# Moving a head's attention scores beside the previous head's values in a decoder layer

## The chip, the cores and the metric

The kernel runs on one core of a Trainium2 chip. The metric is device microseconds of one execution, as the median of several. TensorE (PE) multiplies; ScalarE (ACT), VectorE (DVE) and GpSimd (POOL) do the rest, and SyncE (SP) and POOL issue most transfers.

## The reference

One decoder layer over 256 tokens of width 2048, in float32. The input is normalised and projected. One branch is multi-head latent attention with 16 heads (128 plain and 64 rotary dimensions for queries and keys, 128 for values); the other a gated convolution over three tokens. Both are projected, merged by sigmoid gates, projected once more, normalised and added to the input.

```python
h = _rmsnorm(x, pre_norm_g)
proj = jnp.einsum('bsd,de->bse', h, w_in)
(q_a, c_kv, k_rope, z_mla, c_in, b_gate, c_gate, z_conv, g_mla, g_conv) = jnp.split(proj, cuts, axis=-1)
q = jnp.einsum('bsr,re->bse', _rmsnorm(q_a, q_a_norm_g), w_q_b)
kv = jnp.einsum('bsr,re->bse', _rmsnorm(c_kv, kv_a_norm_g), w_kv_b)
# ... split into heads, rotary positions on q_rope and k_rope
attn = _causal_mla_attention(q_nope, q_rope, k_nope, k_rope, v)
attn = attn.reshape(b, s, MLA_WIDTH) * jax.nn.silu(z_mla)
y_mla = jnp.einsum('bse,ed->bsd', attn, w_o_mla)
u = c_gate * c_in
u_pad = jnp.pad(u, ((0, 0), (CONV_K - 1, 0), (0, 0)))
conv = sum(conv_w[k] * u_pad[:, k:k + s] for k in range(CONV_K))
y_conv = jnp.einsum('bse,ed->bsd', b_gate * conv * jax.nn.silu(z_conv), w_o_conv)
merged = jax.nn.sigmoid(g_mla) * y_mla + jax.nn.sigmoid(g_conv) * y_conv
x = x + _rmsnorm(jnp.einsum('bsd,de->bse', merged, w_out), post_norm_g)
```

## The kernel before

Every float32 product is made from two rounded parts, hi and lo: hi is a copy on ACT, lo the rest of a subtraction on DVE (`split_act`, L242 to L249; the lines L243 and L244 carry most of both engines' work). A product is then three matmuls.

Weights come as a fixed list of units, `plan`, of 1 MB each (2048 columns), numbered in the order of use. `take(i)` (L213) hands out unit i; before that, `ahead` loads units up to three further on and splits the next one. A unit is split in two halves of 1024 columns, into tiles `whi` and `wlo` with five buffers each. So a half can be split only once PE has finished the half five places before it. Loads go through SP's queue.

The middle of the kernel is a loop over the 16 heads (L779 to L855). A head's turn in the loop has four units of the convolution branch, `channels(h, 0)` to `channels(h, 3)`, of 24 matmuls each; they are filler for PE around the attention work and not tied to the head. Four heads make a group with its own four units of `gates` ahead of the first head of the group (`at == 0`). Heads come in pairs: in the first of a pair the rotary queries of the next pair are made (`group_r`), in the second its plain queries and keys (`group_a`).

A head's attention has four steps. `score(h)` (L775) calls `scores` (L599): eight matmuls into the one PSUM bank of tag `st`, then mask, maximum, exponential and sum on DVE and ACT, a transposition into `via` on DVE, and four transfers from POOL's queue into DRAM (`go`). `arrive()` (L772) issues, on POOL's queue, the transfer that brings the oldest waiting tile back (`come`), here the turned probabilities `p`. `turn` (L642) splits them into `pt`, hi on ACT and lo on DVE. `values(h, pt)` (L649) makes four matmuls into the one bank of tag `o`.

Before, `score(h)` stood at the head's start, in front of its first unit (for head 0 behind it; head 15's in head 14 behind the second unit). Its `turn` came in the next head behind the second unit, and `values` behind the third; in a group's first head the previous head's `turn` and `values` stand between the gate units instead.

The convolution's taps (`taps`, L734) shift tokens by transfers on POOL's queue, load three rows of tap weights (`cw`, two buffers) on the same queue, and multiply and add on DVE (L756); `next(tap)` runs the next step. `channels_done` (L709) scales what a head's four units made and so frees the two PSUM banks of tag `cv`.

The program is built with a scheduler that orders each engine's instructions by its own estimate of when they are ready. Matmuls and POOL's transfers keep the order in which they are written. `turn`'s two instructions are pinned behind what was written just before them on their engines (`keep_in_program_order`), but what is written later may still be put in front of them. On the chip each engine runs its queue in the order built.

Of the kernel before, what the change touches and what calls it, by code (L numbers as in the profile page):

```python
# [23 lines left out]
H = 16  # L24
# [58 lines left out]
def tile_layer(ctx: ExitStack, tc: tile.TileContext, xw, w0, xb, x, pos, pvec, post_g, wc, wz, wcv, wkr, wqk, wqr, wv, cwr, wsq, out):  # L83
# [129 lines left out]
    def take(i):  # L213
        ahead(i)
        parts = splits.pop(i)

        def piece(j, n):
            o = j * n
            h, o = o // HALF, o % HALF
            return parts[h][0][:, o : o + n], parts[h][1][:, o : o + n]  # L220

        return piece

    def bank(name, tag="mm", bufs=4):
        return psum.tile([P, 512], F32, name=name, tag=tag, bufs=bufs)
# [80 lines left out]
    def temp(name, shape=(P, S), dt=F32, bufs=2, tag=None):  # L306

        tag, n = tag or name.rstrip("0123456789_"), shape[-1]
        if n % LINE == 0:
            return bp.tile(list(shape), dt, name=name, tag=tag, bufs=bufs)  # L310
        return bp.tile([P, -(-n // LINE) * LINE], dt, name=name, tag=tag, bufs=bufs)[:, :n]
# [78 lines left out]
    def whole(dst, ps):  # L390

        t = temp("half")
        nc.scalar.activation(t[:, :], ps[:, S:], AF.Copy)
        nc.vector.tensor_tensor(dst, ps[:, :S], t[:, :], op=ALU.add)
# [98 lines left out]
    def latent_split(name, both, g):  # L493

        f = lat_f[name].rearrange("p t (i k x) -> p k t i x", i=4, k=KR)
        for k in range(KR):
            hi, lo = (both[:, k, o : o + S].rearrange("p (t i x) -> p t i x", t=NT, i=4) for o in (0, S))
            tc.keep_in_program_order(nc.scalar.activation(hi, f[:, k], AF.Copy, scale=col(g, k)))
            tc.keep_in_program_order(
                nc.vector.scalar_tensor_tensor(lo, f[:, k], col(g, k), hi.bitcast(F32), op0=ALU.mult, op1=ALU.subtract)  # L500
            )
# [33 lines left out]
    def key_rope():  # L535
        rows(kr_f)
        rope(kr_f, kr_f, True)
        split_act(kr[:, 0, :], kr[:, 1, :], kr_f)
# [57 lines left out]
    def make(i, j):  # L596
        {"a": group_a, "r": group_r, "v": group_v}[i](j)
# [44 lines left out]
    def turn(p):  # L642

        pt = temp("pt", (P, 2, 3 * P), F32R, 1)
        hi, lo = (pt[:, j : j + 1, :].rearrange("p o (k q) -> p (o k) q", k=3) for j in range(2))
        split_act(quarters(hi), quarters(lo), by_rows(p[:, :], 3), True)
        return pt

    def values(h, pt):  # L649
        vv = groups["v", h // HV]  # L650
        j = h % HV
        o = bank(f"o{h}", tag="o", bufs=1)
        vs = slice(j * DV, (j + 1) * DV)
        both = o[:, :].rearrange("p (i q) -> p i q", i=2)
        mm = matmul
        mm(both, vv[0][:, 0, vs], pt[:, :, :S], start=True, stop=False)
        mm(o[:, :S], vv[1][:, 0, vs], pt[:, 0, :S], start=False, stop=False)
        mm(o[:, P:S], vv[1][:, 1, vs], pt[:, 0, S:], start=False, stop=False)
        mm(both[:, :, P:], vv[0][:, 1, vs], pt[:, :, S:], start=False, stop=True)

        at = at_t[:, h // HV, :, :].rearrange("p t (i k x) -> p t i k x", i=4, k=HV)[:, :, :, j, :]
        f = temp("f")
        whole(f[:, :], o)
        nc.vector.tensor_tensor(at, f[:, :].rearrange("p (t i x) -> p t i x", t=NT, i=4), at, op=ALU.mult)
# [5 lines left out]
    def quarter(pss, w, i):  # L670

        for t in range(NT):
            for k4 in range(4):
                k = 4 * i + k4
                a = [x_both[:, k, o + t * P : o + (t + 1) * P] for o in (0, S)]
                product(pss[t][:, :], a, w(k4, 512), k == 0, k == KD - 1)

    def gates(v, i):
        if i == 0:
            z_ps["now"] = [bank(f"z{v}_{t}") for t in range(NT)]  # L680
        quarter(z_ps["now"], take(u_gate[v][i]), i)

    def gates_done(v):
        for t in range(NT):
            ps, g, r = z_ps["now"][t], at_t[:, v, t, :], r_col[:, t : t + 1]
            nc.scalar.activation(g, ps[:, :], AF.Sigmoid, scale=r)
            now = nc.vector.scalar_tensor_tensor(g, ps[:, :], r, g, op0=ALU.mult, op1=ALU.mult)
            if v == 0:
                tc.keep_in_program_order(now)

    def gates_turn(v, t):
        g = at_t[:, v, t, :]
        go, come = turned(g, temp("cw", (P, 512), bufs=2), 4)
        go()
        return lambda: come(g)
# [5 lines left out]
    def channels(h, i):  # L701

        if i == 0:
            cv_ps["now"] = [bank(f"cv{h}_{t}", tag="cv", bufs=2) for t in range(NT)]
        quarter(cv_ps["now"], take(u_head[h][i]), i)
        if i == 3:
            channels_done(*divmod(h, 4))

    def channels_done(j, n):  # L709
        for t in range(NT):  # L710
            ps, r = cv_ps["now"][t], r_col[:, t : t + 1]
            w, u = cv_w[:, t, :], cv_t[:, j, t, :]
            if n == 0:
                nc.scalar.activation(u, ps[:, :], AF.Copy, scale=r)
            elif n == 1:
                nc.vector.scalar_tensor_tensor(u, ps[:, :], r, u, op0=ALU.mult, op1=ALU.mult)
            elif n == 2:
                nc.scalar.activation(w, ps[:, :], AF.Copy, scale=r)
            else:
                g = temp("cg", (P, 512), bufs=1)  # L720
                nc.scalar.activation(g[:, :], ps[:, :], AF.Sigmoid, scale=r)
                nc.vector.scalar_tensor_tensor(g[:, :], ps[:, :], r, g[:, :], op0=ALU.mult, op1=ALU.mult)
                nc.vector.tensor_tensor(w, w, g[:, :], op=ALU.mult)
# [48 lines left out]
    def arrive():  # L772
        coming.pop(0)()

    def score(h):  # L775
        ps_by_head[h], come = scores(h)
        coming.append(come)

    for h in range(H):  # L779
        v, at = divmod(h, HV)  # L780

        if at == 0:
            for i in range(4):
                gates(v, i)
                if v == 0 and i == 0:
                    ckv_come()
                elif v == 0 and i == 1:
                    next(table_parts)
                    key_rope()
                elif v == 0 and i == 2:  # L790
                    latent_split("qa", qa, "q_g")
                elif v and i == 0:
                    arrive()
                elif v and i == 1:
                    pt = turn(ps_by_head.pop(h - 1))
                    next(tap)
                elif v and i == 2:
                    values(h - 1, pt)
                    make("v", v)
            if v:  # L800
                next(tap)
            else:
                latent_split("ckv", ckv, "kv_g")
            gates_done(v)
        if h == 0:

            ahead(u_grp["r", 0])
            for i in first:
                make(*i)
            channels(h, 0)  # L810
        if h < H - 1:
            score(h)
        if h:
            channels(h, 0)
        if at == 0:
            coming.append(gates_turn(v, 0))
        channels(h, 1)
        if at == 0:
            arrive()
            coming.append(gates_turn(v, 1))  # L820
        else:
            pt = turn(ps_by_head.pop(h - 1))
        if h == H - 2:
            score(h + 1)

        if at == 2 or h == H - 1:
            next(tap)
        if at and h < H - 1:
            arrive()
        channels(h, 2)  # L830
        if at:
            values(h - 1, pt)
        else:
            arrive()
            if v:
                coming.append(channels_join(v - 1, 0))
        for i in made[h]:
            make(*i)
        if h == H - 1:
            pt = turn(ps_by_head.pop(h))  # L840
        channels(h, 3)
        if at == 2 or h == H - 1:
            next(tap)
        while coming and h < H - 1:
            arrive()
        if h == H - 1:
            values(h, pt)
        if at == 3:
            coming.append(channels_join(v, 1))
        if at == 1:  # L850
            tap = taps(v, 1)
            next(tap)
        elif at == 3 and h + 1 < H or h == H - 2:
            tap = taps(v, 0)
            next(tap)  # L855
# [280 lines left out]
```

## Time and profile before

| | |
|---|---|
| Median of three runs | 1035.57 us (1035.38 to 1036.19) |
| The profiled execution, its time and its span | 1035.04 us and 1033.3 us |
| PE busy, matmuls | 1026.6 us (99%), 4680 |
| DVE, ACT, POOL busy | 682.0 us (66%), 526.5 us (51%), 180.5 us (17%) |
| Mean granted TensorE clock | 0.999 |

Shares are of the span. Times in the views are microseconds from the start of the span; a mean of one instruction is in nanoseconds. A line of a timeline gives start, length, engine, line of the kernel, operation, output and input, and in brackets how long the engine was idle before it and what released it. In a list of groups, the numbers behind the bar are busy time, mean, and idle time before.

### The profile page before, as it was taken

The numbers are of one execution on the slowest core, as the hardware profiler recorded it, in microseconds if no ns is written. First come the engines' busy times: TensorE is split into PE (matmuls) and PEld (weight loads), VectorE is DVE, ScalarE is ACT, GpSimd is POOL, SyncE is SP. The second block draws the span as 40 slices with busy tenths as digits, with TensorE's granted clock in tenths as the row PEclk, the third lists the DMA queues.
The fourth block names the chain that finished last, engine by engine and source line by source line (L and its number), as shares of the span: only waits on it lengthen the run. The fifth ranks groups of instructions, "written<-read, shape, count | busy, mean of one in ns | idle before, by whom it ended". The sixth has DMA issues, their size and how long they took to land.

```text
span 1033.3 us, 12729 instructions
## 1 busy us (share of the span) xinstructions
PE 1026.6 (99%) x4680; PEld 855.2 (83%) x4680; DVE 682.0 (66%) x957; ACT 526.5 (51%) x734; POOL 180.5 (17%) x345
## 2 busy tenths in 40 slices
PE   9999999999999999999999999999999999999997
PEld 7888888888888888888888888888888888888886
DVE  7588777777777677867867785564455455455562
ACT  7766545555455454564555565344434444443551
POOL 4640421104201142112313120020010001002000
PEclk9999999999999999999999999999999999999999
DMA  9775866558665685757776765565566557558642
GB/s 358 282 252 215 274 214 227 205 219 287 193 253 187 209 302 188 282 179 244 251 248 224 262 219 201 203 221 189 202 215 210 189 201 242 180 191 334 232 165 81
DMA packets 44670, 233.25 MB, mean 226 GB/s; under 512 B 7968, under 2 KB 10656, under 8 KB 21696
## 3 DMA queue, kind: packets, MB, share of 16 engines
q1 hardware_dynamic: 32544, 199.67, 54.6%
q0 software_dynamic: 11632, 29.48, 8.5%
q10 hardware_dynamic: 432, 3.29, 0.8%
q8 instruction: 36, 0.59, 0.2%
q14 instruction: 26, 0.21, 0.1%
HBM read 215.66 MB, written 12.58 MB: 221 GB/s over the span
## 4 chain that ended last, share of the span: by engine, by line
PE 99%; DVE 0%; ACT 0%; issue 0%; POOL 0%; POOLq 0%
PE cv L88 34%; PE sq L88 34%; PE out L88 8%; PE z L88 8%; PE qn L88 2%; PE kn L88 2%; PE qa L88 2%; PE vv L88 2%; PE ckv L88 2%; PE sc L88 1%; PE qr L88 1%; PE o L88 1%; PE idle L88 0%; PE kr L88 0%; DVE og L989 0%; ACT junk L970 0%
## 5 line engine op out<-in xcount | busy, mean ns | idle before, releaser
L244 DVE TENSOR_TENSOR wlo<-raw,whi 128x1024 fp32r<-128x1024 f32 (+1 forms) x370 | 440.2, 1196 | 282.4 <-ACT whi L243 271.8
L243 ACT ACTIVATE whi<-raw 128x1024 fp32r<-128x1024 f32 (+1 forms) x372 | 382.6, 1035 | 403.4 <-PE sq L88 180.4
L88 PE MATMUL cv<-whi,x_both 128*128 128x512 f32 x1024 | 321.1, 389 | 0.0
L88 PEld LDWEIGHTS cv<-whi,x_both 128*128 128x128 f32 x1024 | 192.3, 188 | 39.2
L88 PE MATMUL cv<-wlo,x_both 128*128 128x512 f32 x512 | 199.5, 390 | 0.0
L88 PE MATMUL sq<-whi,x_both 128*128 128x512 f32 x512 | 158.3, 389 | 0.0
L88 PEld LDWEIGHTS sq<-whi,x_both 128*128 128x128 f32 x512 | 96.1, 188 | 20.0
L88 PEld LDWEIGHTS cv<-wlo,x_both 128*128 128x128 f32 x512 | 96.2, 188 | 19.0
L88 PE MATMUL sq<-wlo,x_both 128*128 128x512 f32 x256 | 99.6, 389 | 0.0
L88 PE MATMUL z<-whi,x_both 128*128 128x512 f32 x256 | 79.9, 389 | 0.0
L88 PE MATMUL sq<-whi,at_both 128*128 128x512 f32 x256 | 79.5, 389 | 0.0
L88 PE MATMUL sq<-whi,cv_both 128*128 128x512 f32 x256 | 79.5, 389 | 0.0
L88 PE MATMUL out<-whi,m_both 128*128 128x512 f32 x256 | 79.0, 389 | 0.0
L326 POOL DMA_DIRECT2D far<-sg x32 | 17.6, 555 | 312.5 <-DVE sg L318 238.4
L326 POOL DMA_DIRECT2D far<-via x64 | 35.4, 559 | 182.2 <-DVE via L318 182.2
L88 PEld LDWEIGHTS sq<-whi,at_both 128*128 128x128 f32 x256 | 48.1, 188 | 10.0
L88 PEld LDWEIGHTS sq<-whi,cv_both 128*128 128x128 f32 x256 | 48.1, 188 | 10.0
L88 PEld LDWEIGHTS z<-whi,x_both 128*128 128x128 f32 x256 | 48.1, 188 | 10.0
L88 PEld LDWEIGHTS out<-whi,m_both 128*128 128x128 f32 x256 | 48.1, 188 | 9.9
L88 PEld LDWEIGHTS sq<-wlo,x_both 128*128 128x128 f32 x256 | 48.1, 188 | 9.9
L88 PE MATMUL z<-wlo,x_both 128*128 128x512 f32 x128 | 49.8, 389 | 0.0
L88 PE MATMUL sq<-wlo,at_both 128*128 128x512 f32 x128 | 49.8, 389 | 0.0
(217 smaller groups left out, 1126.5 us busy)
## 6 DMA issues: line engine op xcount, KB each, us to landing
raw<-wsq_dram SPq DMA_DIRECT2D x80, 1024.0 KB, 4.8
raw<-wcv_dram SPq DMA_DIRECT2D x64, 1024.0 KB, 5.7
raw<-wz_dram SPq DMA_DIRECT2D x16, 1024.0 KB, 4.8
raw<-wqk_dram SPq DMA_DIRECT2D x8, 1024.0 KB, 6.6
cw<-cwr_dram POOLq DMA_DIRECT2D x24, 256.0 KB, 6.0
raw<-wc_dram SPq DMA_DIRECT2D x4, 1024.0 KB, 10.0
raw<-wv_dram SPq DMA_DIRECT2D x4, 1024.0 KB, 5.1
far<-via POOLq DMA_DIRECT2D x64, 48.0 KB, 3.3
```

Of the source, the lines that this page charges most:

```text
L88: return tc.keep_in_program_order(nc.tensor.matmul(*a, **kw))
L243: a = nc.scalar.activation(hi, src, AF.Copy)
L244: b = nc.vector.tensor_tensor(lo, src, hi.bitcast(F32), op=ALU.subtract)
L326: tc.keep_in_program_order(queue.dma_start(out=f[i], in_=m))
```

## The change

The score of a head moves from its start to behind the third unit of the convolution, in front of the previous head's values. In the first head of a group it moves between the gate units, in front of the same values there, and its transfer back is issued at the end of the gates. Head 0's score moves behind its third unit, head 15's from behind the second unit of head 14 to the end of that head. The transfer back of the other scores, issued before behind the second unit, is now issued at the end of the head (L844's loop), head 15's behind the second unit of head 15.

```diff
@@ the gate units of a group's first head
                     next(tap)
                 elif v and i == 2:
+                    score(h)
                     values(h - 1, pt)
                     make("v", v)
...
             gates_done(v)
+            if v:
+                arrive()
         if h == 0:
...
             for i in first:
                 make(*i)
-            channels(h, 0)
-        if h < H - 1:
-            score(h)
-        if h:
-            channels(h, 0)
+        channels(h, 0)
         if at == 0:
             coming.append(gates_turn(v, 0))
         channels(h, 1)
...
         else:
             pt = turn(ps_by_head.pop(h - 1))
-        if h == H - 2:
-            score(h + 1)
 
         if at == 2 or h == H - 1:
             next(tap)
-        if at and h < H - 1:
+        if h == H - 1:
             arrive()
         channels(h, 2)
+
+        if h == 0 or at and h < H - 1:
+            score(h)
         if at:
             values(h - 1, pt)
...
         while coming and h < H - 1:
             arrive()
+        if h == H - 2:
+            score(h + 1)
         if h == H - 1:
             values(h, pt)
```

## The prediction

> **What bounds the kernel now.** I read the page first: its busy times and the chain that ended last.
>
> ```profile
> span 1033.3 us, 12729 instructions
> PE 1026.6 (99%) x4680; PEld 855.2 (83%) x4680; DVE 682.0 (66%) x957; ACT 526.5 (51%) x734; POOL 180.5 (17%) x345
> PE 99%; DVE 0%; ACT 0%; issue 0%; POOL 0%; POOLq 0%
> ```
>
> PE is busy for 1026.6 of 1033.3 us and carries the chain by itself. Next, the waits of PE alone (engine, line, releaser, total, times, longest):
>
> ```profile
> PE idle L88 <- POOL mhalf L264: 1.0, 1, 1.0
> PE fin L88 <- ACT dg L1011: 0.9, 1, 0.9
> ```
>
> Between the first microsecond and the last product PE waits for nothing. So the change can gain almost nothing: it neither removes nor shortens a matmul, and there is no wait to remove. It can lose wherever something PE needs comes late, and each such wait is paid in full. A microsecond or two (0.2%, 2.1 us) is about what a measurement of this kernel can tell from no change.
>
> The chain in order of time (start, length, what) gives the rhythm around the change:
>
> ```profile
> 245.20 0.94 PE sc L88 x8
> ...
> 291.98 1.40 PE qr L88 x8
> ...
> 316.13 0.57 PE o L88 x4
> ...
> 584.32 5.48 PE cv L88 x24
> 589.80 0.57 PE o L88 x4
> ```
>
> A score (sc) is 0.94 us of PE, a head's values (o) 0.57, a rotary query group (qr) 1.40, a unit of the convolution 5.48. Values need `pt`, the turned probabilities, split on ACT (hi) and then DVE (lo). The timelines of ACT and DVE show how early that is ready today, and the order in which the queues hold it:
>
> ```profile
> 280.24 0.51 ACT L243 ACTIVATE pt<-p 128x384 fp32r<-128x384 f32 x1
> ...
> 316.17 1.06 ACT L243 ACTIVATE whi<-raw 128x1024 fp32r<-128x1024 f32 x1 [0.24 <-PE cv L88]
> ...
> 571.60 1.06 ACT L243 ACTIVATE whi<-raw 128x1024 fp32r<-128x1024 f32 x1 [2.50 <-PE cv L88]
> 572.57 0.51 ACT L243 ACTIVATE pt<-p 128x384 fp32r<-128x384 f32 x1
> ```
>
> ```profile
> 572.69 1.23 DVE L244 TENSOR_TENSOR wlo<-raw,whi 128x1024 fp32r<-128x1024 f32 x1 [1.01 <-ACT whi L243]
> 573.83 0.55 DVE L244 TENSOR_TENSOR pt<-p,pt 128x384 fp32r<-128x384 f32 x1
> ```
>
> The `pt` of 280.24 serves a product some 10 us later. The row at 316.17 is a weight split whose buffer was freed by the unit that PE ended at 316.13: such splits stand in ACT's queue and run 0.04 us after PE lets go. The last two rows of ACT and the two of DVE are the pattern that I price below: a weight split in front of `pt` on both engines. From the start of the first (571.60) to the end of `pt`'s lo part (573.83+0.55 = 574.38) takes 2.78 us.
>
> **The change, part by part.** The PE work is the same to the instruction. In the changed program's built order the score of heads 1 to 14 (bar 4, 8, 12, which get it beside the values in the gate units) stands directly in front of the preceding head's values; head 0's stands behind its third unit, head 15's at the end of head 14. The matmuls' own cost: nothing.
>
> *The time the softmax has.* Before, a score stood at the head's start and its `pt` was turned six units later; now about three units and the group's products lie between. How long the path takes, for the score at 245.20 (DVE, then POOL; the last row is from the answer for tile p):
>
> ```profile
> 242.72 1.71 DVE L460 TENSOR_TENSOR rp_b<-f,sin_t 32x256 f32<-32x256 f32 x4
> ...
> 254.84 0.57 DVE L318 STREAM_TRANSPOSE via<-p 128x384 f32<-128x384 f32 x1
> ```
>
> ```profile
> 255.71 2.20 POOL L326 DMA_DIRECT2D far<-via  x4 [5.54 <-DVE via L318]
> 259.87 0.57 POOL L330 DMA_DIRECT2D p<-far  x1 [1.96 <-DMA far<-via]
> ...
> DMA to landing us min/median/max: 2.7/4.3/6.7
> ```
>
> PE ends that score at 246.14; `via` is done at 255.41 (9.3 us); `p` is sent for at 259.87 and lands 4.3 later (2.7 to 6.7): 18 us in all. (The row at 242.72 is the rotation of a query group, 1.71 us of DVE.) Most turns now have 18 us to the place where they stand and another unit before PE wants them. These are hidden by that unit, 5.48 us. Two places are not, because the queues are fixed when the program is built and the scheduler has put the turn late:
>
> ```
> ACT: ... whi65_0  pt(6)  sc_half(7)  half(o6) ...      DVE: ... wlo65_0  pt(6) ...
> DVE: ... cg(15,1)  wlo115_0  mv1+mv2  cv_w  cv_f*cw  pt(15) ...
> ```
>
> *Heads 2, 6 and 10.* Unit 65 is five half buffers behind head 7's third unit (62), so `whi65_0` can only start when PE ends that unit. PE goes on with sc7 (0.94 us) and then wants o6, which waits for `pt(6)` behind that split on both engines: 0.04 + 2.78 − 0.94 = 1.9 us of waiting. Head 2 (unit 40) and head 10 (unit 90) have the same order: 3 × 1.9 = 5.6 us. This is a lower end, for `p` itself is late here: the built order puts the rotation (1.7 and its two sums), two tap products and the values' sums among the softmax steps on the DVE, some 6 us together, so I count 15.6 us from the score's start to `via` (an estimate), then by the rows above 0.3 + 2.2 + 2.0 + 4.3 to the landing: 24.4. `pt`'s turn comes at 25.7 (0.94 + 0.57 + 1.40 + four units = 24.7, and 1.0 for `whi`). With the slowest landing (6.7) it is 1.1 us more each: 5.6 to 8.9. I take 5.6, the median landing.
>
> *The last values, o15.* PE ends the last convolution unit at 589.80 in both programs, but for the waits above (the same matmuls are before it). What stands in front of `pt(15)`, with its times before (ACT, DVE, POOL timelines, and the page's DMA issues: KB each, median us to landing):
>
> ```profile
> 589.83 0.69 ACT L721 ACTIVATE cg<-cv,r_both 128x512 f32<-128x512 f32 x1 [0.30 <-PE cv L88]
> 590.42 1.05 ACT L243 ACTIVATE whi<-raw 128x1024 fp32r<-128x1024 f32 x1
> ```
>
> ```profile
> 593.25 0.69 DVE L756 TENSOR_TENSOR cv_f<-cv_f,cw 128x512 f32<-128x512 f32 x1
> ```
>
> ```profile
> 571.74 0.52 POOL L747 MEMSET mv<- 1x512 f32 x1 [5.25 <-DVE cv_f L756]
> ...
> 573.77 1.11 POOL L740 DMA_DIRECT2D cw<-cwr_dram  x2
> ...
> cw<-cwr_dram POOLq DMA_DIRECT2D x24, 256.0 KB, 6.0
> ```
>
> Before, `pt(15)` ran in front of all this. Now `pt`'s lo part follows the tap's product with the third `cw` (593.25 before), with two more tap joins of about 0.6 inserted: 593.25 + 1.2 + 0.6 = 595.05, end 595.6. PE waits from 589.80: 5.8 us. On POOL the transfers of head 15's score now stand in front of that tap's transfers. Its score ends on PE at 567.4 (589.80 less four units and o14, 0.57); with 9.3 us to `via`, 0.3 + 2.2 for the four issues and 2.0 for the shift's two fills and copies (571.74 to 573.77), the first `cw` is sent for at 581.3 instead of 573.77 and lands 6.0 later, at 587.3. The third reuses its buffer and waits for the first product (587.9), is sent for at 588.2 to 588.9 and lands near 595: 0.6 us later than the DVE wants it. Sum 6.4, ends 5.8 (the DMA in time) and 8.5 (each landing a us slower).
>
> *The clock.* What a pause of that length does is seen only at the end (PE timeline; windows by columns PE, PEld, DVE, ACT, POOL, granted clock, DMA share, GB/s) and at the start (PE groups):
>
> ```profile
> 1027.35 1.13 PE L88 MATMUL fin<-og,dg 128*128 128x256 f32 x4 [0.87 <-ACT dg L1011]
> ...
> 1031.00:1032.00 1.00, 0.00 (x0) 0.00 (x0) 0.00 (x0) 0.00 (x0) 0.00 (x0) 1.00 0.42 156
> 1032.00:1033.30 1.30, 0.00 (x0) 0.00 (x0) 0.00 (x0) 0.00 (x0) 0.00 (x0) 0.51 0.00 0
> ...
> L88 PE MATMUL idle<-ones 128*128 128x128 f32 x16 | 3.8, 430 | 1.0 <-POOL mhalf L264 1.0
> ...
> L88 PE MATMUL fin<-xr,ident 128*128 128x256 f32 x4 | 1.0, 378 | 0.0
> ```
>
> The last matmul ends at 1028.5; the clock is whole until 1032 and half after it: 3.5 us of idling lose it. The first sixteen matmuls, of 128 columns, take 430 ns each, more than 378 for 256 columns late in the kernel: about 3.8 us at half clock at the start. A 6.4 us wait is longer than 3.5, so I expect half clock behind o15 for about as long as at the start: 3.8 us of work at half speed, 1.9 us lost (ends 0 and 3.8). The waits of 1.9 us lose none. [...] No row here shows a pause in mid-kernel.
>
> *Table loads.* Exponentials now fall between the gates' sigmoids and those of the next head: 18 loads in the built order instead of 12. One load, with the exponential behind it (ACT timeline):
>
> ```profile
> 228.16 1.28 ACT L630 ACT_TABLE_LOAD   x1
> 229.46 0.40 ACT L630 ACTIVATE p<-p,nb 128x128 f32<-128x128 f32 x1
> ```
>
> Six of 1.28 us on ACT, which idles for half of the span; the next instruction starts at once. I take nothing for PE. [...]
>
> *The DVE behind the third unit.* In odd heads the score's steps, 3 us of DVE, now stand in front of the product that frees the convolution's PSUM banks (L716), which the next head's first unit needs:
>
> ```profile
> 275.03 0.74 DVE L716 SCALAR_TENSOR_TENSOR cv_f<-cv,r_both,cv_f 128x512 f32<-128x512 f32 x1
> ```
>
> It ended at 275.77; the second bank is wanted half a unit (2.7) behind 275.05, at 277.8. Spare 2.0 us, and the DVE is idle a third of the span by the page (66% busy) to take up the 3: about 1 us stays, an estimate. Cost 0; 1 us for each of heads 1, 5, 9, 13 if the cover is gone.
>
> Sum: 5.6 + 6.4 + 1.9 = 13.9 us. The profiled execution took 1035.04 (span 1033.3), 0.5 under the median of 1035.57. Against the median: 1049.5 us.
>
> **The rivals.** (1) *The clock stays whole.* The trace shows one loss, at its end, with thin work ahead of it (0.87 us idle before 1027.35); between dense products a pause may have to be longer than 6.4, or mine is shorter than I count. Then 5.6 + 6.4: 1047.6. Against it: 6.4 is well over 3.5.
>
> (2) *More waits.* The crowded DVE also lets the banks (4 us for four heads) or `p` at heads 2, 6, 10 (3.3) come late. 1053 to 1057; with the first price 1053.5. For it: spares of about 1 us worked out by hand; against it: weights are split two units ahead.
>
> (3) *Not slower.* `pt` comes in time, as the row at 280.24 shows for today, and PE never waits. It would need DVE and ACT to do `pt` before the splits that stand in front of it, that is, those splits freed at least 1.9 us earlier and o15's chain 5.8 us earlier. The time is then that of before, less what a change of shape between products might cost: a score's 1920 columns at the convolution's pace (5.48 us for 24 x 512) are 0.86 us, 0.08 under its 0.94, 1.3 for sixteen: 1034.3. The built order speaks against it; nothing but an error in my reading of it speaks for it.
>
> (4) *The turns alone*, with o15's chain in time: 1041.2. Against it: `pt(15)` is behind a split that PE itself frees at 589.80.
>
> **How the numbers follow.** Forecast 0.48; rival 1 0.22; rival 2 0.18; rival 4 0.06; rival 3 0.06. The range reaches from rival 1 with one turn in time and the short o15 wait (3.7 + 5.8: 1045.0) to rival 2 with half of each price (1049.5 + 2 + 1.6) and the slow end of o15 (2.1), 1055.5; outside lie rivals 3, 4 and the tail of 2. Slower by over 0.2%: 0.93; rival 3 is mostly within 0.2% (0.05); faster by more (0.02) has no wait to come from.
>
> **What would show it.** The waits of PE, empty today, should name DVE's L244 for o: three of about 1.9 us near 182, 318 and 454 (right behind the scores of heads 3, 7 and 11) and one of about 6 us from about 595 on. The granted clock should be below 1 for a few us behind the last. PE's busy time should grow by no more than the half-clock stretch; table loads by six. I am wrong if PE's waits stay empty, if they sit at weight splits (whi, wlo) or at cv's first matmul instead of o, or if the long one is under 3 us.

## The result

| | before | after |
|---|---|---|
| Median of six executions each | 1035.70 us (1035.38 to 1036.78) | 1051.72 us (1051.24 to 1053.91) |
| The profiled execution and its span | 1035.04 us, 1033.3 us | 1051.91 us, 1050.1 us |

The ratio after to before is 1.0159 (95% interval 1.0148 to 1.0170): slower by 16.0 us. The forecast was 1049.5 with a range from 1045.0 to 1055.5.

The page of the changed kernel, its busy times and the chain that ended last:

```profile
PE 1030.9 (98%) x4680; PEld 857.6 (82%) x4680; DVE 680.7 (65%) x957; ACT 535.4 (51%) x740; POOL 179.6 (17%) x345
PE 89%; POOL 3%; DVE 3%; issue 3%; ACT 1%; DVEq 0%; POOLq 0%; ACTq 0%
```

The same 4680 matmuls, six more instructions on ACT (the table loads), and PE no longer carries the chain alone. Its waits (engine, line, releaser, total, times, longest):

```profile
PE o L88 <- DVE pt L244: 11.9, 4, 5.8
PE idle L88 <- POOL mhalf L264: 1.0, 1, 1.0
PE fin L88 <- ACT dg L1013: 0.9, 1, 0.9
PE cv L88 <- DVE wlo L244: 0.4, 1, 0.4
```

The second and third were there before. New are the last, 0.4 us of which more below, and the first; PE's timeline gives its four places: the values of heads 2, 6, 10 and 15 wait for `pt`.

```profile
184.85 0.54 PE L88 MATMUL o<-pt,vv_hi 128*128 128x512 f32 x1 [2.04 <-DVE pt L244]
...
323.03 0.47 PE L88 MATMUL o<-pt,vv_hi 128*128 128x512 f32 x1 [2.04 <-DVE pt L244]
...
459.63 0.47 PE L88 MATMUL o<-pt,vv_hi 128*128 128x512 f32 x1 [2.04 <-DVE pt L244]
...
604.69 0.76 PE L88 MATMUL o<-pt,vv_hi 128*128 128x512 f32 x1 [5.81 <-DVE pt L244]
```

The queues of ACT and DVE in front of o6 (323.03) show why:

```profile
320.10 1.06 ACT L243 ACTIVATE whi<-raw 128x1024 fp32r<-128x1024 f32 x1 [0.24 <-PE cv L88]
321.07 0.51 ACT L243 ACTIVATE pt<-p 128x384 fp32r<-128x384 f32 x1
```

```profile
319.89 2.53 DVE L244 TENSOR_TENSOR wlo<-raw,whi 128x1024 fp32r<-128x1024 f32 x2 [2.86 <-ACT whi L243]
322.34 0.55 DVE L244 TENSOR_TENSOR pt<-p,pt 128x384 fp32r<-128x384 f32 x1
```

ACT idles 0.24 us until PE gives up a buffer, splits the weights, and only then `pt`; on DVE `pt` stands behind the halves of `wlo`, and PE starts 0.14 us after `pt`'s lo part ends (322.89). In front of o15 on ACT and DVE:

```profile
601.47 0.52 ACT L243 ACTIVATE pt<-p 128x384 fp32r<-128x384 f32 x1 [0.92 <-DMA p<-far]
```

```profile
601.05 1.21 DVE L244 TENSOR_TENSOR wlo<-raw,whi 128x1024 fp32r<-128x1024 f32 x1
602.19 0.68 DVE L756 TENSOR_TENSOR mv<-mv,mv 128x512 f32<-128x512 f32 x1
602.79 0.68 DVE L723 TENSOR_TENSOR cv_w<-cv_w,cg 128x512 f32<-128x512 f32 x1
603.39 0.68 DVE L756 TENSOR_TENSOR cv_f<-cv_f,cw 128x512 f32<-128x512 f32 x1
603.99 0.55 DVE L244 TENSOR_TENSOR pt<-p,pt 128x384 fp32r<-128x384 f32 x1
```

DVE is busy without a gap; the product with the third `cw` (603.39) does not wait for its transfer. ACT does wait for `p`, 0.92 us, but its part of `pt` ends at 601.99, two microseconds before DVE comes to the other.

The rest of the loss is the clock (windows: stretch, length, PE, PEld, DVE, ACT, POOL, granted clock, DMA share, GB/s):

```profile
185.00:186.00 1.00, 1.00 (x5) 0.93 (x6) 0.96 (x4) 0.00 (x0) 0.00 (x0) 0.56 0.96 401
186.00:187.00 1.00, 1.00 (x4) 0.81 (x3) 0.52 (x3) 0.38 (x1) 0.00 (x0) 0.50 1.00 426
...
188.00:189.00 1.00, 1.00 (x5) 0.82 (x4) 0.89 (x4) 0.00 (x1) 0.00 (x0) 0.73 0.00 0
189.00:190.00 1.00, 1.00 (x10) 1.00 (x9) 0.40 (x1) 0.82 (x1) 0.31 (x1) 1.00 0.00 0
...
601.00:602.00 1.00, 0.00 (x0) 0.00 (x0) 1.00 (x2) 0.52 (x1) 0.00 (x0) 0.77 0.69 164
...
608.00:609.00 1.00, 1.00 (x5) 0.81 (x4) 0.20 (x1) 0.00 (x0) 1.00 (x3) 0.81 0.43 98
```

A slice wholly inside a stretch reads 0.50, one outside 1.00; a slice with a clock of 0.56 was at half speed for 0.88 us of it. So the clock was halved from 185.12 to 188.54, right behind the pause before o2, and from 601.54 to 608.38, from the middle of the pause before o15. The first costs 3.42 / 2 = 1.7 us; of the second only the part behind 604.69 counts, 3.69 / 2 = 1.85 us. The pauses before o6 and o10, with 2.04 us as long as the one before o2, lost no clock (1.00 from 321 to 329 and from 457 to 464).

Where the 16.8 us between the two spans arise can be read by comparing where the same products start in PE's two timelines:

| first product of | before | after | later by |
|---|---|---|---|
| o0 | 127.83 | 129.09 | 1.26 |
| o4 | 262.33 | 267.27 | 4.94 |
| o8 | 396.83 | 403.87 | 7.04 |
| o12 | 531.33 | 540.47 | 9.14 |
| the last | 1027.35 | 1044.20 | 16.85 |

To o4: 3.7, a wait of 2.04 and 1.7 of clock. To o8 and o12: 2.1 each, a wait. To the end: 7.7, a wait of 5.81 and 1.85 of clock. Ahead of o0: 1.3, of which 0.3 comes before the first convolution product, 0.4 is a wait that the list names (cv for `wlo`), and the other 0.5 has no row of its own.

### The profile page after: what moved, and what is told of

Same layout as the page of the kernel before. It is cut to its first block, busy times and chain, and to the rows that moved or that the text cites. A ratio compares the mean times of both kernels' runs of the same rounds, so it can differ in the third digit from the quotient of the medians.

```text
span 1050.1 us, 12730 instructions
## 1 busy us (share of the span) xinstructions
PE 1030.9 (98%) x4680; PEld 857.6 (82%) x4680; DVE 680.7 (65%) x957; ACT 535.4 (51%) x740; POOL 179.6 (17%) x345
## 4 chain that ended last, share of the span: by engine, by line
PE 89%; POOL 3%; DVE 3%; issue 3%; ACT 1%; DVEq 0%; POOLq 0%; ACTq 0%
PE sq L88 33%; PE cv L88 33%; PE out L88 8%; PE z L88 6%; PE qn L88 2%; PE kn L88 2%; PE vv L88 2%; PE sc L88 1%; PE o L88 1%; DVE wlo L244 1%; PE qr L88 1%; POOL ta_y L408 1%; POOL ta_r L411 1%; POOL cos_t L445 1%; ACT whi L243 1%
## 5 line engine op out<-in xcount | busy, mean ns | idle before, releaser
L88 PEld LDWEIGHTS sq<-wlo,x_both 128*128 128x128 f32 x256 | 48.3, 189 | 10.1
L88 PEld LDWEIGHTS out<-whi,m_both 128*128 128x128 f32 x256 | 48.0, 188 | 10.1
```

The lines of the kernel that those rows point to most:

```text
L88: return tc.keep_in_program_order(nc.tensor.matmul(*a, **kw))
```

## The experiments

Each kernel below ran on one chip with the kernel before, whose median there was 1035.6 to 1035.7; "after" is 1051.7.

### Heads 2, 6 and 10 back at their start (e2_old_2610)

```diff
+        if h in (2, 6, 10):
+            score(h)
         channels(h, 0)
...
-        if h == H - 1:
+        if h == H - 1 or h in (2, 6, 10):
             arrive()
         channels(h, 2)
-        if h == 0 or at and h < H - 1:
+        if (h == 0 or at and h < H - 1) and h not in (2, 6, 10):
             score(h)
```

> The scores of heads 2, 6 and 10 go back to the start of their head; heads 3, 7 and 11 and the last two keep the changed place. Theory (these three moves cost three waits of 2.04 us and, behind o2, half clock worth 1.7): the waits at o3, o7 and o11 in the trace go, 6.1 us, with 0.7 of slow first products and the 1.7 of clock: 1051.7 - 6.1 - 0.7 - 1.7 = 1043.2; if the half clock comes at random and not in most executions, 1045. Rival (the time is lost by all moved heads alike, through more work on ScalarE and VectorE beside the convolution): a fifth of the 16 us per score in proportion, three of fifteen, 3.2: 1048.5.

Measured: 1052.61 (1050.32 to 1054.57). Neither theory: the three waits for `pt` were gone, and three others of the same length had come. PE's waits and its timeline:

```profile
PE sc L88 <- DVE kn L244: 6.4, 3, 2.1
```

```profile
143.36 0.36 PE L88 MATMUL sc<-kn,qn_hi 128*128 128x256 f32 x1 [2.14 <-DVE kn L244]
```

DVE's queue in front of it:

```profile
141.00 1.23 DVE L244 TENSOR_TENSOR wlo<-raw,whi 128x1024 fp32r<-128x1024 f32 x1 [1.03 <-ACT whi L243]
142.14 0.74 DVE L716 SCALAR_TENSOR_TENSOR cv_f<-cv,r_both,cv_f 128x512 f32<-128x512 f32 x1
142.80 0.75 DVE L244 TENSOR_TENSOR kn<-f,kn 128x256 fp32r<-128x256 f32 x2
```

The keys `kn` of head 2 are split behind a weight split that PE frees late, the pattern of `pt` once more. With head 1's score moved and head 2's not, head 1's softmax steps run on DVE from 130.94 to 136.87, in the stretch in which head 2's keys are made, and the keys' split ends up behind that of the weights. In the next experiment, in which head 1's score is back at its start too, the keys' split (139.83) stands in front of the weights' (141.62). A place that is harmless in the kernel before need not be harmless beside a neighbour that has moved.

### Both scores of those pairs back (e8_old_pairs)

The same edit with a longer list, at its three places:

```diff
-        if h in (2, 6, 10):
+        if h in (1, 2, 5, 6, 9, 10):
             score(h)
```

> The scores of heads 1 and 2, 5 and 6, 9 and 10 go back to the start of their head; 3, 4, 7, 8, 11 to 15 and 0 keep the changed place. With only 2, 6 and 10 back, each of them had waited 2.1 us for kn, behind the steps of the score in front of it, which stood one unit earlier. Theory (that wait comes from the short distance of two scores, one moved and one not): with both back there is neither a wait for pt at o2, o6, o10 nor one for kn: 1051.7 less 6.1, less 0.7 of slow first products, less the half clock that such a pause sometimes brings (1.7 in the trace of the changed kernel): 1043.2 to 1044.9. Rival (VectorE and ScalarE have too much to do beside these heads wherever the scores stand): waits of some 2 us turn up at head 3, 7 and 11, and 1049 or more.

Measured: 1044.75 (1044.01 to 1045.36), 7.0 less than after, inside the expected 1043.2 to 1044.9. No wait for `pt` is left but o15's of 5.8, and none for `kn`. So the three waits, with the half clock that one of them brings, are 7.0 of the 16.0 us. By the trace of the changed kernel they are 7.8 (6.1 and 1.7); part of the difference lies in the clock behind o15, which in this trace is halved until 602.60, 5.1 us behind o15's start (597.47), and so costs 2.6 in place of 1.85.

### The split of p first, at heads 2, 6 and 10 (e1_pin)

```diff
-            pt = turn(ps_by_head.pop(h - 1))
+            pt = turn(ps_by_head.pop(h - 1), u_gate[v + 1][0] if at == 3 and v + 1 < NV else None)
...
     def split_unit(i):
+        with behind(i):
+            split_now(i)
```

`turn` keeps its two instructions under the number of a unit; `behind` lets nothing of that unit's split be queued ahead of them.

> Only the order on ScalarE and VectorE is changed: in front of values 2, 6 and 10 the split of p (pt, L244) is queued ahead of the split of the next group's first weights (whi and wlo, for which TensorE is waited for). Nothing is taken out or added. Theory (the place in the queue makes the waits): p of head 6 landed near 320.6 in the trace of the changed kernel and o6 was wanted at 320.99, so pt's two parts would be done near 321.7 and each of the three waits drops from 2.04 us to 0.7 or less; the half clock behind o2 (1.7 us lost) goes too. Time 1045.5 to 1048. Rival (p itself comes late, the queue is an excuse): the waits stay at 2.0 and the time at 1051.7. A second rival: the weights, now split later, make convolution or value products wait, and TensorE shows waits on whi or wlo in place of pt; time 1050 to 1053.

Measured: 1049.00 (1048.85 to 1049.56), 2.7 less than after. The waits fell to 1.34, 1.33 and 1.26, not to 0.7, and the clock was whole at all three (its mean is 0.996, against 0.994 in the changed kernel). PE's and ACT's timelines at o6:

```profile
320.74 0.47 PE L88 MATMUL o<-pt,vv_hi 128*128 128x512 f32 x1 [1.33 <-DVE pt L257]
```

```profile
319.48 0.52 ACT L256 ACTIVATE pt<-p 128x384 fp32r<-128x384 f32 x1 [1.21 <-DMA p<-far]
```

With nothing in front of it `pt` now waits 1.21 us for `p` itself. Score 6 started at 293.62, so `p` landed 25.9 us later. DVE's last row of the path and POOL's rows show which part was longer than counted:

```profile
308.56 0.57 DVE L332 STREAM_TRANSPOSE via<-p 128x384 f32<-128x384 f32 x1
```

```profile
309.43 2.22 POOL L340 DMA_DIRECT2D far<-via  x4 [17.29 <-DVE via L332]
315.14 0.57 POOL L344 DMA_DIRECT2D p<-far  x1 [3.50 <-DMA far<-via]
```

`via` is done 15.5 us after the score's start, as estimated (15.6), and `p` lands 4.3 after it is sent for, as counted; but the four transfers into DRAM keep POOL waiting for 3.5 us, not 2.0. What makes them slower than in the row of the kernel before was not tried. The queue's order made 0.7 us of each wait; behind it stood a transfer that would have made 1.3 anyway. Both theories hold in part. Shorter waits (2.2 us in all) and the whole clock behind o2 (1.7) would make 3.9 and not 2.7 us: in this trace o0 comes 0.7 later (129.75 against 129.09), and the clock behind o15 costs 0.3 more.

### The last two scores at their old places (e3_old_tail)

```diff
+        if h == H - 2:
+            score(h)
         channels(h, 0)
...
+        if h == H - 2:
+            score(h + 1)
         if at == 2 or h == H - 1:
             next(tap)
...
         while coming and h < H - 1:
             arrive()
-        if h == H - 2:
-            score(h + 1)
```

> The scores of the last two heads, 14 and 15, stand where the kernel before had them; all others keep the changed place. Theory (the late score of head 15 costs 5.8 us of wait and 2.0 us of half clock behind it): one wait less and a whole clock from 595 on: 1051.7 - 5.8 - 2.0 - 0.2 = 1043.7. Rival 1 (the clock behind the long wait is not lost through the wait, only by chance of the profiled execution): 1045.7 to 1046. Rival 2 (the wait moves to the next late thing, the value products of head 14 or the third table of the rotated taps): 1047 or more, with a wait of TensorE on another tile.

Measured: 1047.77 (1047.45 to 1047.96), 3.95 less than after. Rival 2 by its number: o15's wait and its half clock were gone, and another wait had come, on `kn`:

```profile
PE sc L88 <- DVE kn L244: 2.1, 1, 2.1
```

It is head 14's score at 554.09, with half clock behind it from 554.45 to 557.86 (1.7): the pair effect of the first experiment, here with head 13 moved and 14 not. 5.8 + 1.85 − 2.1 − 1.7 = 3.85.

### p(15) sent for ahead of the third table (e5_come_first)

```diff
+        if h == H - 1:
+            arrive()
         if at == 2 or h == H - 1:
             next(tap)
-        if h == H - 1:
-            arrive()
```

> In the last head the transfers that bring p(15) are sent for ahead of the third table of the tap (cw) instead of behind it; with that the split of p(15) also moves up on VectorE, in front of the tap's products with cw, but stays behind the split of the weights 115_0 on both engines. Theory (two things keep o15 waiting: the tap's work and the transfer behind cw, then the weights' split that TensorE frees only at 598.87): the first goes, the second stays, so o15's wait falls from 5.8 to about 4.6 us (split of 115_0 done 602.2, one joined step 0.6, p's lo part 0.55) and the time to 1050.4. Rival 1 (the transfer of p alone decides): wait near 0 and 1043.7. Rival 2 (neither, something else ends last): 5.8 and 1051.7.

Measured: o15 waited 4.61 us, as the theory said; 1051.05 (1050.34 to 1052.34), with the profiled execution at 1050.34. The medians alone don't separate this kernel from after; the wait does.

### Split of p(15) ahead of unit 115 (e6_tail)

The edit of e5_come_first, and the split of p(15) pinned (as in e1_pin) ahead of unit 115's, of head 15's `channels_done` and of the tap's last step:

```diff
-            pt = turn(ps_by_head.pop(h))
+            pt = turn(ps_by_head.pop(h), u_d[0][0][2])
+            pins["last"] = pins[u_d[0][0][2]]
         channels(h, 3)
-        if at == 2 or h == H - 1:
-            next(tap)
+        with behind("last"):
+            if at == 2 or h == H - 1:
+                next(tap)
```

> As the kernel with p(15) sent for first, and besides the split of p(15) is queued on ScalarE and VectorE ahead of the split of weights 115_0, of the channels' last joins and of the tap's last products. No work is taken out or added. Theory (queue places alone make o15's wait): p(15) lands near 595.5 and its split ends by 597.5, before o15 is wanted at 598.9, so the wait of 5.8 and the half clock behind it (2.0) go: 1051.7 - 5.8 - 2.0 - 0.2 = 1043.7. Rival 1 (p(15) itself lands late, as p did by 0.6 us at the earlier heads): a wait of 1 to 2 us stays, 1045 to 1046. Rival 2 (the work pushed back makes the next products late): the time comes back at the weights of unit 115 or at the last tap, 1047 or more.

Measured: 1048.94 (1047.81 to 1051.81); o15 waited 2.94. Neither the theory nor a rival had the reason. ACT split `p` at 597.31 without a wait for its transfer; DVE's timeline shows the rest:

```profile
597.44 1.22 DVE L257 TENSOR_TENSOR wlo<-raw,whi 128x1024 fp32r<-128x1024 f32 x1 [1.97 <-ACT whi L256]
598.58 0.68 DVE L771 TENSOR_TENSOR mv<-mv,cw 128x512 f32<-128x512 f32 x1
599.30 0.69 DVE L771 TENSOR_TENSOR mv<-mv,mv 128x512 f32<-128x512 f32 x1
599.91 0.55 DVE L257 TENSOR_TENSOR pt<-p,pt 128x384 fp32r<-128x384 f32 x1
```

Between `pt`'s two parts stand half a weight split of unit 114 and two steps of the tap, which I had not moved.

### Split of p(15) ahead of all of them (e11_tail_first)

The edit of e6_tail with two differences: the split is pinned ahead of that of unit 114, which comes before 115's, and the tap's step with the first two tables is written behind it. Lines marked as removed are those of e6_tail or, for `turn`, of the changed kernel.

```diff
-        if at == 2 or h == H - 1:
+        if at == 2:
             next(tap)
...
-            pt = turn(ps_by_head.pop(h))
+            pt = turn(ps_by_head.pop(h), u_d[0][0][1])
+            pins["last"] = pins[u_d[0][0][1]]
+            with behind("last"):
+                next(tap)
```

> The last head's tail once more: p(15) is sent for first, and its split is queued ahead of the splits of units 114 and 115, of the tap's products with all three tables and of the channels' last joins. The trace with the split ahead of unit 115 alone had left 2.9 us: p was there, but VectorE had the second half of 114's split and two joined products of the tap in front of pt (597.44 to 599.91). Theory (queue places alone make o15's wait): pt is done 1 us after p lands near 594.5, before o15 is wanted at 597.7 to 598.9; no wait, no half clock at the end: 1051.7 - 5.8 - 2.0 - 0.2 = 1043.7. Rival 1 (the transfer of p decides too): a wait of 1 us or more for pt. Rival 2 (what was pushed back is wanted soon): waits on unit 114's or 115's weights, 1045 or more.

Measured: 1044.28 (1044.02 to 1044.90), 7.4 less than after, and whole clock from 190 to the end. ACT's and PE's timelines:

```profile
597.67 0.53 ACT L256 ACTIVATE pt<-p 128x384 fp32r<-128x384 f32 x1 [4.05 <-DMA p<-far]
```

```profile
598.93 0.47 PE L88 MATMUL o<-pt,vv_hi 128*128 128x512 f32 x1 [0.26 <-DVE pt L257]
```

ACT waits for `p` itself, and PE for 0.26 us more. So the order of the queues, POOL's and those of ACT and DVE, made all but 0.26 of o15's 5.8 us in this trace. And `p` is only just in time: sent for at 590.66, it was there for its split 7.0 us later.

### All splits of p first (e12_all_first)

The edits of e1_pin and e11_tail_first together, all sixteen scores at the changed place.

> The same tail, and the splits of p(2), p(6) and p(10) queued ahead of the weights' splits as well; all sixteen scores keep the changed place. Theory: what is left over the kernel before are three waits of 1.3 us, in which p itself is late, their slow first products (0.24 each) and about 0.5 to 0.8 for the first weights of the convolution: 1035.7 + 3.9 + 0.7 + 0.6 = 1040.9, with the clock whole, since no pause reaches 2 us. Rival (the half clock follows any pause over 1 us in some executions): 1041.5 to 1044, with a spread over 1.5 us between executions.

Measured: 1041.59 (1041.44 to 1041.99), 10.1 less than after: the 2.7 and the 7.4 of the two pins, added. The clock was whole throughout (its mean is 0.999, that of the kernel before), with four pauses of 1.34, 1.35, 1.45 and 0.84 us. At o15 the same pins leave 0.84 here and 0.26 in e11_tail_first: `p`, sent for at 587.62, was there for its split at 595.23, 7.6 us later. Against the kernel before 6.0 us are left: these 5.0, in which `p` itself is late, and about 0.9 of which the experiments at the end speak. No order of the queues that I tried wins the change back.

### PE kept busy while it waits (e4_warm)

```diff
+        for _ in range({2: 8, 6: 8, 10: 8, 15: 24}.get(h, 0)):
+            mm(o[:, :], x_both[:, 0, :P], x_both[:, 0, :], start=True, stop=True)
         mm(both, vv[0][:, 0, vs], pt[:, :, :S], start=True, stop=False)
```

> Products of 128 columns on data that lie in SBUF since the start are added ahead of values 2, 6 and 10 (8 each) and of the last values (24); their results are overwritten by the values' own first products. The split of p comes as late as before, so the waits of o become shorter by what the added products take, and TensorE idles for less than 1.7 us or so at a time. Theory (the waits cost more than their length, because TensorE loses its clock behind them): the 1.7 us behind o2 and the 2.0 us behind the last values come back, 1051.7 - 3.7 = 1048. Rival (the clock in these places has nothing to do with the pauses): half clock in the same places and 1051.7. If the added products themselves hold the values back, 1052 to 1053.

Measured: 1049.04 (1048.80 to 1050.19), 2.7 less than after although 48 products were added. The windows around o2 and o15, with a whole clock:

```profile
180.00:190.00 10.00, 9.90 (x53) 8.21 (x53) 6.55 (x16) 5.66 (x12) 0.00 (x0) 1.00 0.55 215
...
595.00:610.00 15.00, 14.72 (x67) 11.92 (x66) 12.67 (x21) 5.21 (x8) 4.30 (x8) 1.00 0.69 222
```

The same `pt` came as late as before (the first real product of o15 starts at 604.73, against 604.69), so in these two places it is the idling of PE that halves the clock: busy for 9.90 of 10 us and 14.72 of 15 it has 1.00, in the changed kernel, busy for 7.96 and 9.19, it has 0.83 and 0.77. Against the expected 3.7 us 1.0 is missing; 0.7 of it may be a new row in PE's waits:

```profile
PE cv L88 <- ACT cv_f L716: 0.7, 1, 0.7
```

The first unit of head 13 waits here (525.93) for its second PSUM bank, which head 12's scaling on ACT frees (L714 in the changed kernel, two lines further down here). It is not one of the places where I had counted a spare of 1 us: there it is DVE that frees the bank, behind a score's steps. In front of this row ACT had stood 2.25 us waiting for the transfer of a weight unit (to 518.98). The profiled execution, at 1050.19, is the slowest of the four; whether the others have this wait is open.

### What moves for nothing (e10_third_only, e13_six_only, e14_six_only)

In the first, only heads 0, 3, 4, 7, 8, 11 and 12 keep the changed place; the other two take head 0 away as well, in e13 ahead of the convolution's first unit, in e14 behind it, where the kernel before has it. The edit of e10 is that of e3 with more heads; e14 adds two lines:

```diff
+        if h in (1, 2, 5, 6, 9, 10, 13) or h == H - 2:
+            score(h)
         channels(h, 0)
+        if h == 0:
+            score(h)
```

In e13 the number 0 joined the list above instead.

> As with the pairs back, and the scores of heads 13, 14 and 15 too: only 0, 3, 4, 7, 8, 11 and 12 keep the changed place. Theory (moving costs nothing by itself; only the heads whose p is wanted soon behind the move pay): no wait of TensorE for pt or kn, whole clock: 1035.7 to 1036.5, up to 0.8 over the kernel before for the first weights of the convolution, which wait 0.4 to 0.8 now that head 0's score no longer stands in front of them. Rival 1 (each move costs about the same): seven fifteenths of 16 us, 1043. Rival 2 (scores at the convolution's pace save 0.08 each): 1035.2, within what can be measured of the kernel before.

Measured: 1036.18, ratio 1.0004 (0.9995 to 1.0013). 8.6 us less than with the pairs back: the tail's share (in the trace with the pairs back, 5.8 of wait and 2.6 of clock). PE's new wait:

```profile
PE cv L88 <- DVE wlo L244: 0.5, 1, 0.5
```

> Only the scores of heads 3, 4, 7, 8, 11 and 12 keep the changed place; head 0's too goes back to the start of its head. Theory (with head 0's score away from the front of the convolution, the first weights there came 0.5 us late): no wait on wlo near 92, and 1035.7, or 1035.2 if scores at the convolution's pace save anything. Rival (the difference of 0.5 between the kernel with seven moved and the kernel before is scatter): 1036.2 again.

Measured: 1039.73, a trial of a place that I had misread. PE's timeline shows the score waiting for the rotary queries, with half clock from 90.65 to 94.06 behind it (2.87 + 1.7 = 4.6):

```profile
90.50 0.47 PE L88 MATMUL sc<-kr,qr 128*128 128x256 f32 x1 [2.87 <-DVE qr L244]
```

> The scores of heads 3, 4, 7, 8, 11 and 12 alone keep the changed place. Head 0's score stands where it stood, behind the first unit of its convolution; the last trial had put it ahead of that unit, a place in which neither kernel has it, and there it waited 2.9 us for qr. Theory (the 0.5 us by which the kernel with seven moved scores was above the kernel before is the wait of the first convolution products for wlo near 92, which head 0's score hides in its old place): no wait of TensorE but those of the kernel before, 1035.2 to 1035.8. Rival 1 (scatter, or a cost of the six moves): 1036.2. Rival 2 (scores at the convolution's pace save 0.08 us each, half a us for six): 1035.1 or less.

Measured: 1035.32 (11 executions) against 1035.69 (15), ratio 0.9997 (0.9988 to 1.0006). PE waits as before, but for 0.3 at the start:

```profile
PE idle L88 <- POOL mhalf L264: 1.0, 1, 1.0
PE fin L88 <- ACT dg L1017: 0.9, 1, 0.9
PE qa L88 <- ACT whi L243: 0.3, 1, 0.3
```

So six of the moves cost nothing that can be measured, and head 0's costs 0.9 by the medians (1036.18 less 1035.32; their intervals against the kernel before overlap) and 0.6 by the two traces, from the first product of the convolution to o0 (42.23 against 41.59). If scores at the convolution's pace save anything, it is at the edge: from o0 to the last product this trace takes 899.23 against 899.52, 0.05 per move. A kernel that is measurably faster than the one before was not found.

## Why the prediction was right

**What bounds the kernel.** Right: PE had no wait to lose, and each new wait was paid in full, the short ones (2.1 us later for each 2.04, to o8 and to o12) and the long one. It was not all that was paid, see the clock.

**Heads 2, 6 and 10.** Right in place and cause: 3 × 2.04 instead of 3 × 1.88. The split from `whi` to the end of `pt` took 2.79 (320.10 to 322.89), as counted; the 0.14 from there to PE's start was not in the sum. My landing of `p` (24.4 us after the score's start) was short: 25.9 in e1_pin, the wait for the four transfers into DRAM. It did not show, since the split stood in front of it; but with `pt` first, 1.3 of each wait stays. "A lower end" was the right word for the term.

**o15.** Forecast 6.4, measured 5.81, the lower end named. The mis-sized step is the third `cw`: I had it land 0.6 later than DVE wants it, and it was in time: sent for at 597.14, it was there when DVE came to it at 603.39, so within 6.25 us. The places in the queue were as read (e5, e6 and e11 take them away one by one: 5.8, 4.6, 2.9, 0.3).

**The clock.** The 1.9 us behind o15 was 1.85, in part by luck: I had the half clock begin with o15 and last as long as at the start, but it began in the middle of the wait and lasted 6.8 us. Behind waits of the same 5.8 us the traces of e2, e1 and e8 lose 1.7, 2.1 and 2.6. The step that failed is "the waits of 1.9 us lose none": the pause before o2 was followed by 3.4 us at half speed, 1.7 us that the sum lacked. I had taken the 3.5 us of idling at the kernel's end for the length that a pause must have.

**Terms at zero.** Table loads: right, 18 of them and no wait of PE behind one. ACT's timeline shows the next instruction start where the load ends:

```profile
271.50 1.28 ACT L630 ACT_TABLE_LOAD   x1
272.79 0.40 ACT L630 ACTIVATE p<-p,nb 128x128 f32<-128x128 f32 x1
```

The PSUM banks of the convolution: right, no such wait in the changed kernel, nor in any other trace at the four places that I named; the wait in e4_warm is for a bank that ACT frees. Not on my list at all: head 0's score, moved, no longer covers the split of the convolution's first weights, 0.6 to 0.9 us by e10 and e14.

**The sum.** 13.9 forecast, 16.0 measured. In the medians of the experiments: 7.0 for the three pairs, 8.6 for the tail, 0.9 for head 0; these add up to 16.4 because e14 lies 0.4 under the kernel before. The forecast missed by 2.2 us, and the terms differ by 1.7 (half clock behind o2), 0.9 (head 0's cover), 0.5 (short waits) and −0.6 (`cw`): 2.5. Two slips of adding in the forecast change nothing here: the prices named for the range's upper end make 1055.2 and not 1055.5, and four units with the three terms ahead of them 24.8 and not 24.7.

**The rivals.** Rival 1 fell with the clock. Rival 2 (banks and `p` late at heads 2, 6 and 10) did not show in the changed kernel; the late `p` came up where an experiment took its cover away (e1), the late banks nowhere. Rivals 3 and 4 fell with PE's waits: the three short ones and o15's are all there.

## What to carry to other kernels

When a step is moved closer to its consumer, ask not how long its path takes but what stands in front of it in the in-order queues of its helper engines, and which of those things the consumer's own engine frees: a split that waits for PE's last buffer, ahead of the operand PE wants next, made PE wait 2.04 us each time here, from the 2.79 of the splits on both engines less the 0.94 of a score in between. Count such waits of TensorE with a surcharge for the clock: of the 19 of 2.03 to 2.14 us in these traces 5 cost about 1.7 us more, and the 2.94 of e6_tail cost 3.1 more. And look at neighbours: putting one of two steps back gave the same wait in another place.

## What the runs showed that I had not expected

Pauses of the same length did not cost the same. The two half-clock stretches of the changed kernel begin 416.42 us apart and last 3.42 and 6.84 us, the second twice as long as the first. Neither begins where its pause begins or ends: behind the pause before o2 the clock was halved 0.27 us after PE had started again, at o15 3.15 us before it did (601.54 against 604.69). Half clock came with five pauses of 2.03 to 2.14 us (after, e2, e3 twice, e11), with the 2.87 us of e13 and with the waits of 2.94 to 5.83 before o15, and with none of the pauses of 0.84 to 1.45 in e1 (at heads 2, 6 and 10) and e12. Four pauses of about 2 us, times from the start of each span:

| trace, wait of | pause | its length | half clock |
|---|---|---|---|
| after, o2 | 182.82 to 184.85 | 2.04 | from 185.12 |
| e2, head 2's score | 141.22 to 143.36 | 2.14 | from 144.74 |
| e6_tail, o10 | 456.39 to 458.43 | 2.04 | none |
| after, o10 | 457.60 to 459.63 | 2.04 | none |

In e2 PE's rows show it: a product with `wlo` takes 0.63 us at 145.77 and 147.05, and 0.39 at 148.26. In e6_tail the clock is whole around the pause before o10; at o15 it is half from 599.97, before PE starts again at 600.61, to 606.80:

```profile
457.00:458.00 1.00, 0.00 (x0) 0.00 (x0) 1.00 (x2) 0.14 (x1) 0.00 (x0) 1.00 0.60 90
458.00:459.00 1.00, 0.57 (x4) 0.56 (x5) 1.00 (x5) 0.00 (x0) 0.00 (x0) 1.00 0.73 262
459.00:460.00 1.00, 1.00 (x8) 0.84 (x7) 0.84 (x4) 0.38 (x1) 0.00 (x0) 1.00 1.04 442
460.00:461.00 1.00, 1.00 (x6) 0.84 (x5) 0.58 (x3) 0.77 (x3) 0.00 (x0) 1.00 0.61 254
461.00:462.00 1.00, 1.00 (x10) 1.00 (x9) 0.71 (x3) 1.00 (x3) 0.00 (x0) 1.00 0.00 0
599.00:600.00 1.00, 0.00 (x0) 0.00 (x0) 0.96 (x3) 0.99 (x3) 0.00 (x0) 0.98 0.53 131
600.00:603.00 3.00, 2.39 (x7) 2.13 (x8) 3.00 (x5) 1.25 (x3) 0.00 (x0) 0.50 0.86 322
603.00:606.00 3.00, 3.00 (x8) 2.31 (x7) 2.93 (x6) 0.58 (x1) 0.00 (x0) 0.50 0.04 14
606.00:607.00 1.00, 1.00 (x4) 0.78 (x3) 1.00 (x3) 0.00 (x0) 0.00 (x0) 0.60 0.00 0
```

```profile
458.43 0.47 PE L88 MATMUL o<-pt,vv_hi 128*128 128x512 f32 x1 [2.04 <-DVE pt L257]
```

So a pause of 2 us cost 2 us or 3.7: of 19 such pauses in six traces, 5 lost the clock, 14 did not. What decides between them is not shown; no run shifted one pause in small steps. And once halved, the clock did not come back as soon as PE was busy: in e6_tail it stayed half for 6.2 us of work without a pause. The start differs between executions too: the first four products of `qa` take 1.18 us in e14 and 2.08 in e4, and the first product of the convolution starts at 86.33 and 87.24. Part of the scatter of a microsecond between executions of one kernel may come from there (not tried).
